# First experts of a two-block transformer layer: 24 rounds of 128 slots on 32-column strips, float32 unsplit, with an 18-slab weight ring

## Chip, cores and metric

The program runs on one core of a Trainium2 chip. The metric is the device time of one execution in microseconds; the kernel before has a median of 3347.88 us over three runs (3345.87 to 3349.38).

## What is computed

The reference is a layer of two blocks over 1024 tokens of width 1024 (256 context tokens beside them). The change is in the experts of the first block. After the mixer every token has a row of `h2`, chooses one of four groups of experts, and inside it two of eight experts:

```python
def hier_moe(h, w_rg, b_rg, w_re, b_re, w_gate, w_up, w_down):
    """h (T, D): top-1 expert group, then top-2 experts inside that group; SwiGLU experts."""
    ...
    def expert_block(args):
        xi, e = args
        return (jax.nn.silu(xi @ w_gate[e]) * (xi @ w_up[e])) @ w_down[e]
    ...
x = x + gt2 * hier_moe(h2.reshape(B * S, D), *moe_args).reshape(B, S, D)
```

There are 32 experts, each with `w_gate` and `w_up` of 1024x512 and `w_down` of 512x1024, all float32: 192 half matrices of 1 MB each. The 1024 tokens give 2048 rows of work. Block 2 (a recurrent branch, attention, and 64 experts of 256 hidden columns) follows and isn't changed.

## The kernel before, in words

The kernel is written with a tile framework that has pools of buffers and inserts the semaphore waits; its scheduler sets the order of each engine's instructions. It goes through the mixer of block 1 (`phase1a`, `phase1b`, `phase1c`), the 32 experts of block 1 (`moe1`, the place of the change), the mixer of block 2 (`phase3`) and its 64 experts (`moe2`).

**Routing.** `route_group` runs twice in `phase1c` (for token tiles 0 to 5, then 6 and 7). It gives every token-and-choice a slot number in its expert (`slot`, L832 to L833), builds one-hot rows of it (`rsl`, L859) and accumulates, with small products, a table of 96 slots x 32 experts in PSUM. `finish_table` (L876 to L881) copies it out and makes `o_tok` (token of each slot, or a negative number) and `o_w` (its weight). An expert's first 96 slots are handled in `moe1`; what lies beyond goes to `overflow`, a loop with a trip count read at run time (L1059, L1060), which is zero for these inputs: its body never runs, but all engines and DMA queues meet at a barrier there.

**Experts.** `moe1` goes through the experts one at a time, R = 96 slots each. `fetch(e)` gathers 96 rows of `h2d` into one of three buffers `m_x` (an indirect DMA of the POOL queue, L1009); `front(e)` turns them with eight transposes (L999) and splits them in two float32r parts, `m_xTh` and `m_xTl` (L1002, L1003). Weights come in slabs of 128x2048 float32 (1 MB, six to an expert: gate and up in halves of the contraction, down in halves) by DMAs of the SP queue (L1155) into a ring of 8 buffers `m_w`. `split(j)` makes two float32r parts of each slab: `m_hi` on ACT (L1179) and `m_lo` on DVE, for the second half of down on POOL (L1180); four buffers each. `mm3` then does each float32 product as three float32r products (hi x hi, lo x hi, hi x lo), 128x96 stationary (the turned rows) against 512 moving columns of the slab:

```python
    def product(out, x, w, k, o, start, stop):
        self.mm3(out[0:R], x[0][:, k, :], x[1][:, k, :], w[0][:, o:o + 512], w[1][:, o:o + 512], start, stop)
    ...
    def taken():
        j = step[0]
        step[0] += 1
        split(j + 4)
        load(j + 4 + self.M1_RING)
```

So an expert is 72 products: 48 for gate and up (`ph`), 24 for down (`py`). Silu and the product with up give `m_h` (L1254, L1255); it is turned with four transposes and multiplied with down while the next expert's gate and up run. DVE scales the result with weight and gate (`m_y`, L1226), and an indirect DMA of POOL adds its rows to `x1d` (`scatter`, L1015). After expert 20's gate and up stands `overflow`.

**After the experts**, `phase3` starts with `norms`: SP loads the gain `g`, weights `wzs` and `ws` of `w_in`, `fg` (L1444, L1280, L1448), and the rows `a_x` of `x1d` (L1451), which have to wait for the last scatter.

**moe2**, whose code stays as it is, handles two experts at a time: 64 slots of one on columns 0 to 63 of the TensorE array, 64 of the other on columns 64 to 127, in float32 unsplit (`n_w`, `n_d` the weights). In `phase1a` the small products of the modulation (`ad<-wada,cT`) put four 32-column stationary operands on the four 32-column strips of the array, float32 unsplit, in eight products to a result.

## Time and profile before

| | us |
|---|---|
| median of 3 runs | 3347.88 |
| lowest, highest run | 3345.87, 3349.38 |
| span of the profiled execution | 3342.7 |
| the execution's median beside its span | 5.2 more |
| PE busy in the span | 2993.7 (90%) |
| DVE, ACT, POOL busy | 1768.0, 1370.7, 835.8 |
| first to last product of the block-1 experts | 982.9 to about 1648 |
| `moe2` | about 2783 to the end |

The profiled execution has no run time of its own in the results; its span of 3342.7 us is taken as the median run less 5.2 us that lie around the span. A row of a view gives start or count, busy time and mean duration; "idle before" is the engine's idle time just before the instruction and who ended it. PE is the matmul part of TensorE, PEld its weight loads, SPq the queue on which SP issues DMAs.

### The profile page before, as it was taken

To read this page: it belongs to the slowest core of one execution; us is meant where nothing else is said; L and a number is where in the kernel's file an instruction comes from. 1 tells how busy PE (TensorE), PEld (TensorE's weight loads), DVE (VectorE), ACT (ScalarE), POOL (GpSimd) and SP (SyncE) were. 2 spreads that over 40 slices of the span, in tenths; PEclk is the share of its full clock that TensorE was granted. 3 is DMA by queue.
4 is the path that set the end of the run, shared out by engine and by line. 5 is a ranking of instruction groups with operands and counts; after the bars stand their busy time and mean duration, and the time that the engine had idled before them with its cause. 6 is when DMAs were issued, how large, how long until landed. Compare 5 with 4: busy or idle time off the path is not lost.

```text
span 3342.7 us, 42770 instructions
## 1 busy us (share of the span) xinstructions
PE 2993.7 (90%) x15849; PEld 2195.4 (66%) x15849; DVE 1768.0 (53%) x3374; ACT 1370.7 (41%) x2247; POOL 835.8 (25%) x553
## 2 busy tenths in 40 slices
PE   7999999799978899889799999999998997877858
PEld 4988854677756666666487778788887893332323
DVE  4244332877668778778656731348886443111101
ACT  4345311555535566566556632236664211000001
POOL 1000011122223468767510000110001103333332
PEclk8999999799989899999899999999999998999979
DMA  6223376666569899899732253332235549999988
GB/s 212 91 80 95 92 226 198 178 166 173 137 225 317 285 330 343 285 359 343 234 118 76 76 208 96 120 96 73 69 83 179 178 173 346 407 386 363 390 334 301
DMA packets 282097, 705.55 MB, mean 211 GB/s; under 512 B 33760, under 2 KB 168060, under 8 KB 233116
## 3 DMA queue, kind: packets, MB, share of 16 engines
q1 hardware_dynamic: 231036, 462.13, 42.3%
q0 software_dynamic: 44160, 222.81, 18.4%
q10 hardware_dynamic: 6688, 17.83, 1.5%
q8 instruction: 127, 2.08, 0.3%
q14 instruction: 86, 0.70, 0.1%
HBM read 616.11 MB, written 99.11 MB: 214 GB/s over the span
## 4 chain that ended last, share of the span: by engine, by line
PE 41%; DMA 17%; DVE 9%; POOL 5%; ACT 4%; issue 4%; POOLq 0%; SPq 0%; DVEq 0%; ACTq 0%
PE mm L88 31%; DMA n_d<-exp_w 13%; POOL m_lo L1180 3%; PE s L88 2%; PE tp L88 2%; ACT m_hi L1179 2%; DVE m_lo L1180 1%; DMA x1d<-m_y,o_tok 1%; PE tp L999 1%; PE o L88 1%; PE gt L88 1%; PE tp L691 1%; PE lg L88 1%; DVE da_e L660 1%; POOL m_rs L101 1%
## 5 line engine op out<-in xcount | busy, mean ns | idle before, releaser
L1180 DVE TENSOR_TENSOR m_lo<-m_w,m_hi 128x2048 fp32r<-128x2048 f32 x160 | 430.3, 2703 | 78.9 <-ACT m_hi L1179 70.3
L1179 ACT CAST m_hi<-m_w 128x2048 fp32r<-128x2048 f32 x192 | 360.6, 1907 | 84.4 <-PE mm L88 74.0
L88 PE MATMUL mm<-n_w,n_xTf 128*64 128x512 f32 x1024 | 271.6, 645 | 79.5 <-DMA n_w<-exp_w 58.1
L88 PEld LDWEIGHTS mm<-n_w,n_xTf 128*64 128x64 f32 x1024 | 92.3, 149 | 252.7 <-issue 250.3
L88 PE MATMUL mm<-m_lo,m_xTh 128*96 128x512 f32 x512 | 205.5, 401 | 20.0 <-DVE m_lo L1180 19.9
L88 PE MATMUL mm<-m_hi,m_xTh 128*96 128x512 f32 x512 | 206.9, 404 | 0.0
L88 PE MATMUL mm<-uTh,wh 128*128 128x512 f32 x512 | 205.3, 401 | 0.0
L88 PE MATMUL mm<-m_hi,m_xTl 128*96 128x512 f32 x512 | 204.4, 399 | 0.0
L88 PE MATMUL mm<-uTh,wl 128*128 128x512 f32 x512 | 203.2, 397 | 0.0
L88 PE MATMUL mm<-uTl,wh 128*128 128x512 f32 x512 | 202.4, 395 | 0.0
L88 PE MATMUL mm<-wh,hTh 128*128 128x256 f32 (+1 forms) x608 | 177.6, 292 | 2.0 <-ACT wh L269 2.0
L1284 DVE TENSOR_TENSOR wl<-ws,wh 128x512 fp32r<-128x512 f32 x128 | 91.5, 729 | 164.9 <-ACT wh L1283 152.2
L88 PE MATMUL mm<-wl,hTh 128*128 128x256 f32 (+1 forms) x608 | 175.5, 289 | 0.5 <-DVE wl L270 0.5
L88 PE MATMUL mm<-wh,hTl 128*128 128x256 f32 (+1 forms) x608 | 175.1, 288 | 0.6 <-DVE hTl L324 0.6
L1967 DVE TENSOR_TENSOR n_h<-n_h,mm 128x256 f32<-128x256 f32 x32 | 13.5, 420 | 304.4 <-ACT n_h L1966 304.4
L1180 POOL TENSOR_TENSOR m_lo<-m_w,m_hi 128x2048 fp32r<-128x2048 f32 x32 | 159.6, 4989 | 52.0 <-ACT m_hi L1179 46.3
L1009 POOL DMA_INDIRECT m_x<-h2d,o_tok x32 | 129.2, 4038 | 156.3 <-PE tp L999 129.0
L1015 POOL DMA_INDIRECT x1d<-m_y,o_tok x32 | 149.8, 4681 | 48.8 <-DVE m_y L1226 42.7
L1966 ACT ACTIVATE n_h<-mm 128x256 f32<-128x256 f32 x32 | 12.3, 384 | 327.6 <-PE mm L88 327.6
L88 PE MATMUL mm<-m_lo,m_hTh 128*96 128x512 f32 x256 | 104.3, 420 | 34.8 <-POOL m_lo L1180 34.8
L88 PE MATMUL s<-da_k,da_q 128*128 128x512 f32 (+1 forms) x384 | 115.0, 409 | 17.7 <-DVE da_e L660 17.3
L1283 ACT CAST wh<-ws 128x512 fp32r<-128x512 f32 x128 | 77.7, 619 | 127.2 <-PE mm L88 51.5
(534 smaller groups left out, 7653.4 us busy)
## 6 DMA issues: line engine op xcount, KB each, us to landing
n_w<-exp_w POOLq DMA_DIRECT2D x112, 1024.0 KB, 16.9
m_w<-expert_w_gate SPq DMA_DIRECT2D x64, 1024.0 KB
m_w<-expert_w_up SPq DMA_DIRECT2D x64, 1024.0 KB
m_w<-expert_w_down SPq DMA_DIRECT2D x64, 1024.0 KB
n_d<-exp_w POOLq DMA_DIRECT2D x58, 1024.0 KB, 16.8
wada<-w_ada SPq DMA_DIRECT2D x48, 512.0 KB
da_k<-ks SPq DMA_DIRECT2D x64, 320.0 KB
n_w<-exp_w SPq DMA_DIRECT2D x12, 1024.0 KB
```

The lines of the kernel that those rows point to most:

```text
L88: self.nc.tensor.matmul(out, l, r, start=start, stop=stop)
L101: nc.gpsimd.tensor_tensor(out, m, self.neghalf[:, 0:w], op=ALU.pow)
L660: nc.vector.tensor_scalar(e[:, c0:c0 + n], ps, 0.125, mx[:, m, b - 1:b] if b else None, op0=ALU.mult, op1=ALU.max, accum_out=mx[:, m, b:b ...
L691: nc.tensor.transpose(pt[:, i, :], e[:, ts(4 * g + i, P)], self.ident)
L999: nc.tensor.transpose(pt[:, k, :], xk[:, g + k, :], self.ident[0:rows, 0:rows])
L1009: return self.nc.gpsimd.indirect_dma_start(out=out, out_offset=None, in_=src, in_offset=bass.IndirectOffsetOnAxis(ap=idx, axis=0), bounds_ ...
L1015: return self.nc.gpsimd.indirect_dma_start(out=dst, out_offset=bass.IndirectOffsetOnAxis(ap=idx, axis=0), in_=src, in_offset=None, bounds_ ...
L1179: nc.scalar.copy(hi, w)
L1180: (nc.gpsimd if order[j][1] == 5 else nc.vector).tensor_tensor(lo, w, hi.bitcast(F32), op=ALU.subtract)
L1283: nc.scalar.copy(wh[:, r, :], st)
L1284: nc.vector.tensor_tensor(wl[:, r, :], st, wh[:, r, :].bitcast(F32), op=ALU.subtract)
L1967: nc.vector.tensor_tensor(h, h, ph[:, 1, :], op=ALU.mult)
```

## The change

The 32 experts are taken as 24 rounds of 128 slots. A round is four strips of 32 slots; strip q of round r belongs to expert `expert(r, q)`: three rounds handle four experts (one of each group of experts), three strips each. A strip's 32 turned rows are the stationary operand on 32 columns of the array, and its result lands on 32 partitions of the PSUM bank; so four experts' strips (of two different experts) stand side by side. Products are float32 unsplit (`turn_cols` with split False, no `mm3`), and `split` is gone. Experts of groups 1 and 2 are used in two rounds that follow each other, and a slab is given back after its last use (`left`). The ring has 18 slabs: 8 in the pool that held it before and 10 in the pool of `moe1`, where `m_hi` and `m_lo` lay. Gather, scatter and the DVE and ACT steps have 128 rows. The table of routing gets rows by round (`first`, `row`) and is copied out in seven pieces, on DVE and ACT in turn. `overflow` comes after round 15 of 24. Comments and docstrings are taken out, so line numbers move.

```diff
@@ route_group
+        row, rows = slot, cap
+        if "first" in out:
+            row, rows = self.t(pool, [P, 2, GT], tag="rrow")[:, :, 0:g], P
+            for k, oh in enumerate((oh0, oh1)):
+                nc.vector.tensor_tensor(tmp, oh, out["first"].unsqueeze(1).to_broadcast([P, g, E]), op=ALU.mult)
+                nc.vector.tensor_reduce(row[:, k, :], tmp, axis=AX.X, op=ALU.add)
+            past = self.t(pool, [P, 2, GT], tag="rpast")[:, :, 0:g]
+            nc.vector.tensor_tensor(row, row, slot, op=ALU.add)
+            nc.vector.tensor_scalar(past, row, 128.0, -128.0, op0=ALU.is_ge, op1=ALU.mult)
+            nc.vector.tensor_tensor(row, row, past, op=ALU.add)
+            nc.vector.tensor_scalar(past, slot, float(cap), 1000.0, op0=ALU.is_ge, op1=ALU.mult)
+            nc.vector.tensor_tensor(row, row, past, op=ALU.add)
...
-                nc.vector.tensor_scalar(sl[:, 0:cap], self.mats[:, 7, 0:cap], slot[:, k, t - t0:t - t0 + 1], None, op0=ALU.is_equal)
+                nc.vector.tensor_scalar(sl[:, 0:rows], self.mats[:, 7, 0:rows], row[:, k, t - t0:t - t0 + 1], None, op0=ALU.is_equal)
                 for u in range(nsub):
-                    self.mm(tab[u * cap:(u + 1) * cap], sl[:, 0:cap], fields[:, :, k, t - t0, u * (E // nsub):(u + 1) * (E // nsub)],
+                    self.mm(tab[u * rows:(u + 1) * rows], sl[:, 0:rows], fields[:, :, k, t - t0, u * (E // nsub):(u + 1) * (E // nsub)],
                             t == 0 and k == 0, t == NT - 1 and k == 1)
         if t1 == NT:
-            self.finish_table(pool, tab, out["tok"], out["w"], E // nsub, nsub * cap)
@@ finish_table
+        if rounds:
+            to, of = tb.rearrange("p f (j i) -> p f j i", i=3), tab.rearrange("p f (g j) -> p f j g", g=4)
+            for i, g, r0, r1 in ((0, 0, 0, 96), (0, 1, 96, 128), (1, 1, 0, 64), (1, 2, 64, 128), (2, 2, 0, 32), (2, 3, 32, 64), (2, 3, 64, 128)):
+                (nc.vector.tensor_copy if g % 2 else nc.scalar.copy)(to[r0:r1, :, :, i], of[r0:r1, :, :, g])
+        else:
+            nc.vector.tensor_copy(tb, tab[0:n])
...
@@ route_tiles
+        more = {}
+        if rounds:
+            n = 3 * E // 4
+            more["first"] = self.t(pool, [P, E], tag="o_first")
+            for g in range(4):
+                self.nc.gpsimd.memset(more["first"][:, ts(g, E // 4)], float(self.cap1 * g % P))
+        return more | {
             "cnt": self.t(pool, [P, E], tag="o_cnt"),
@@ moe1_open, moe1_load, moe1
-    M1_RING = 8
+    M1_RING = (8, 10)
     def moe1_open(self, wp):
...
-        order = [(0, 0), (0, 1)]
-        for e in range(E):
-            if e:
-                order += [(e, 0), (e, 1), (e - 1, 4), (e - 1, 5)]
-            order += [(e, 2), (e, 3)]
-        self.m1_order = order + [(E - 1, 4), (E - 1, 5)]
-        self.m1_slabs, self.m1w = {}, wp
-    def moe1_load(self, j):
+        order, before = [], None
+        for r in range(24):
+            s, i = divmod(r, 3)
+            new = [(8 * g + s) for g in ((0, 1), (2,), (3,))[i]]
+            for h in range(2):
+                order += [(e, 2 * h + j) for j in range(2) for e in new]
+                if h == 0 and before:
+                    order += [(e, 4 + j) for j in range(2) for e in before]
+            before = new
+        self.m1_order = order + [(e, 4 + j) for j in range(2) for e in before]
+        self.m1_slabs, self.m1w, self.m1_next = {}, [wp], 0
+    def moe1_load(self):
         nc, a = self.nc, self.a
...
-        e, i = self.m1_order[j]
+        e, i = self.m1_order[self.m1_next]
+        at = self.m1_next % sum(self.M1_RING)
+        self.m1_next += 1
...
-        w = self.m1_slabs[j] = self.t(self.m1w, [P, 2048], tag="m_w", bufs=self.M1_RING)
+        ring = int(at >= self.M1_RING[0])
+        w = self.m1_slabs[e, i] = self.t(self.m1w[ring], [P, 2048], tag=f"m_w{ring}", bufs=self.M1_RING[ring])
         nc.sync.dma_start(w, src.rearrange("p k n -> p (k n)"))
     def moe1(self, rt):
-        E, HID, R = 32, 512, self.cap1
+        E, HID, ROUNDS = 32, 512, 24
...
+            self.m1w.append(pool)
             gt2 = self.t(pool, [P, D], tag="gt2")
             nc.gpsimd.dma_start(gt2, self.rows[3:4, :].to_broadcast([P, D]))
-            slabs, order, load, parts, xTs = self.m1_slabs, self.m1_order, self.moe1_load, {}, {}
+            slabs, order, xTs = self.m1_slabs, self.m1_order, {}
+            left = {(e, i): 1 + (e // 8 in (1, 2)) for e, i in order}
             xbuf = []
...
-            def split(j):
-                if j >= len(order):
-                    return
-                w = slabs.pop(j)
-                hi = self.t(pool, [P, 2048], F32R, tag="m_hi", bufs=4)
-                lo = self.t(pool, [P, 2048], F32R, tag="m_lo", bufs=4)
-                nc.scalar.copy(hi, w)
-                (nc.gpsimd if order[j][1] == 5 else nc.vector).tensor_tensor(lo, w, hi.bitcast(F32), op=ALU.subtract)
-                parts[order[j]] = (hi, lo)
-            def fetch(e):
-                if e < E:
-                    self.gather(xbuf[e % 3][0:R], self.h2d, rt["tok"][0:R, e:e + 1], S - 1)
-            def front(e):
-                if e < E:
-                    xTs[e] = self.turn_cols(pool, psum, xbuf[e % 3], 8, "m_xT", True, R)
-            def product(out, x, w, k, o, start, stop):
-                self.mm3(out[0:R], x[0][:, k, :], x[1][:, k, :], w[0][:, o:o + 512], w[1][:, o:o + 512], start, stop)
...
-            def taken():
-                j = step[0]
-                step[0] += 1
-                split(j + 4)
-                load(j + 4 + self.M1_RING)
-            def gate_up(e, i, ph):
-                w = take((e, i))
+            def expert(r, q):
+                s, i = divmod(r, 3)
+                return 8 * ((4 * i + q) // 3) + s
+            def fill():
+                while self.m1_next < len(order) and (
+                        self.m1_next < sum(self.M1_RING) or not left[order[self.m1_next - sum(self.M1_RING)]]):
+                    self.moe1_load()
+            def taken(r, i):
+                for e in {expert(r, q) for q in range(4)}:
+                    left[e, i] -= 1
+                fill()
+            def fetch(r):
+                if r < ROUNDS:
+                    self.gather(xbuf[r % 3], self.h2d, rt["tok"][:, r:r + 1], S - 1)
+            def front(r):
+                if r < ROUNDS:
+                    xTs[r] = self.turn_cols(pool, psum, xbuf[r % 3], 8, "m_xT", False)
+            def gate_up(r, i, ph):
                 for k in range(4):
                     kk = 4 * (i // 2) + k
-                    product(ph[i % 2], xTs[e], w, kk, 512 * k, kk == 0, kk == 7)
-                taken()
-            def turn_h(e, h):
-                return self.turn_cols(pool, psum, h, 4, "m_hT", True, R)
-            def down(e, hT):
+                    for q in range(4):
+                        self.mm(ph[i % 2][ts(q, 32)], xTs[r][:, kk, ts(q, 32)], slabs[expert(r, q), i][:, ts(k, 512)], kk == 0, kk == 7)
+                taken(r, i)
+            def down(r, hT):
                 y = self.t(pool, [P, D], tag="m_y", bufs=2)
                 py = [self.t(psum, [P, 512], tag="mm", bufs=6) for c in range(2)]
                 for i in range(2):
-                    w = take((e, 4 + i))
                     for k in range(2):
                         for c in range(2):
-                            product(py[c], hT, w, 2 * i + k, 1024 * k + 512 * c, i + k == 0, i + k == 2)
-                    taken()
+                            for q in range(4):
+                                w = slabs[expert(r, q), 4 + i]
+                                self.mm(py[c][ts(q, 32)], hT[:, 2 * i + k, ts(q, 32)], w[:, 1024 * k + 512 * c:1024 * k + 512 * c + 512],
+                                        i + k == 0, i + k == 2)
+                    taken(r, 4 + i)
...
-                self.scatter(self.x1d, rt["tok"][0:R, e:e + 1], y[0:R])
-            for e in range(3):
-                fetch(e)
-            with tc.manual_schedule(engines={mybir.EngineType.DVE}):
-                split(0)
-                load(self.M1_RING)
-                front(0)
-                for j in range(1, 4):
-                    split(j)
-                    load(j + self.M1_RING)
+                self.scatter(self.x1d, rt["tok"][:, r:r + 1], y)
+            for r in range(3):
+                fetch(r)
+            fill()
+            front(0)
...
-                gate_up(e, 0, ph)
-                if e:
-                    hT = turn_h(e - 1, h)
-                gate_up(e, 1, ph)
-                if e:
-                    down(e - 1, hT)
-                    fetch(e + 2)
-                front(e + 1)
-                gate_up(e, 2, ph)
-                gate_up(e, 3, ph)
-                xTs.pop(e)
+                gate_up(r, 0, ph)
+                if r:
+                    hT = self.turn_cols(pool, psum, h, 4, "m_hT", False)
+                gate_up(r, 1, ph)
+                if r:
+                    down(r - 1, hT)
+                    fetch(r + 2)
+                front(r + 1)
+                gate_up(r, 2, ph)
+                gate_up(r, 3, ph)
+                xTs.pop(r)
                 h = self.t(pool, [P, HID], tag="m_h", bufs=2)
-                nc.scalar.activation(h[0:R], ph[0][0:R], AF.Silu)
-                nc.vector.tensor_tensor(h[0:R], h[0:R], ph[1][0:R], op=ALU.mult)
-                if e == 20:
+                nc.scalar.activation(h, ph[0], AF.Silu)
+                nc.vector.tensor_tensor(h, h, ph[1], op=ALU.mult)
+                if r == 15:
                     self.overflow(pool, psum, "m_", rt, self.h2d, self.x1d, wg.rearrange("e d h -> (e d) h"),
...
-            down(E - 1, turn_h(E - 1, h))
+            down(ROUNDS - 1, self.turn_cols(pool, psum, h, 4, "m_hT", False))
```

In the order of instructions the change shows at three places.

SP, around the end of `phase1c` (x1d and h2d are the last stores of the mixer, `m_w` the slabs). Before:

```order
L759 DMA x1d_1033_5561<-c_x_1947_8960 128x1024 [waits DMAHW5_49,DVE_49]
L768 DMA h2d_1034_5562<-c_h_1952_9019 128x1024 [waits DMAHW6_49,Pool_49]
L1059 TENSOR_LOAD v_ni_2649_12307 [waits DVE_49]
L1059 ISA x2
L1155 DMA m_w_1992_9182<-expert_w_gate 128x2048 [waits DMAHW7_49,DVE_49]
L1155 DMA m_w_1999_9204<-expert_w_up 128x2048 [waits DMAHW0_49,DVE_49,Activation_49]
```

Now:

```order
L759 DMA x1d_1033_5561<-c_x_1950_8976 128x1024 [waits DMAHW5_49,DVE_49]
L768 DMA h2d_1034_5562<-c_h_1955_9035 128x1024 [waits DMAHW6_49,Pool_49]
L1188 DMA m_w1_1995_9209<-expert_w_gate 128x2048 [waits DMAHW7_49,PE_49]
L1188 DMA m_w1_1996_9211<-expert_w_up 128x2048 [waits DMAHW0_49]
L1188 DMA m_w1_1997_9213<-expert_w_down 128x2048 [waits DMAHW1_49,DVE_49,DMAHW5_49,PE_49,Activation_49]
L1188 DMA m_w1_1998_9215<-expert_w_down 128x2048 [waits DMAHW6_49,DMAHW2_49]
```

The ninth slab no longer stands behind a register load that waits for the routing's last DVE step, nor for DVE's and ACT's splits; ten slabs follow the store of `h2d` directly. Up to the barrier of `overflow` SP now issues 137 of the 192 loads.

SP, at the end of the experts (`g1`, `wzs1152` and `fg` are the first loads of `phase3`, `a_x` the rows of x1d). Before:

```order
L1155 DMA m_w_3024_14032<-expert_w_down 128x2048 [waits DMAHW6_49,DVE_49]
L1444 DMA g1_3088_14319<-norm1_g_2 128x1024 [waits DMAHW7_49]
L1280 DMA wzs1152_3091_14323<-w_in_2 128x4x288 [waits DMAHW0_49]
L1280 DMA wzs1152_3092_14327<-w_in_2 128x4x288 [waits DMAHW1_49]
L1280 DMA wzs1152_3095_14333<-w_in_2 128x4x288 [waits DMAHW2_49]
L1448 DMA fg_3087_14318<-final_norm_g 128x1024 [waits DMAHW3_49]
L1280 DMA wzs1152_3096_14337<-w_in_2 128x4x288 [waits DMAHW4_49,DMAHW0_49,DVE_49]
L1451 DMA a_x_3078_14309<-x1d_1033_5561 128x1024 [waits DMASW3_49,DMAHW5_49,PE_49,Pool_49]
```

Now:

```order
L1188 DMA m_w1_2518_12906<-expert_w_down 128x2048 [waits DMAHW6_49]
L1463 DMA g1_2557_13133<-norm1_g_2 128x1024 [waits DMASW3_49,DMASW5_49,DMASW2_49,DMASW7_49,DMASW1_49,DMAHW7_49,DMASW0_49,DVE_49]
L1299 DMA wzs1152_2560_13137<-w_in_2 128x4x288 [waits DMAHW0_49]
L1299 DMA wzs1152_2561_13141<-w_in_2 128x4x288 [waits DMAHW1_49]
L1299 DMA wzs1152_2564_13147<-w_in_2 128x4x288 [waits DMAHW2_49]
L1467 DMA fg_2556_13132<-final_norm_g 128x1024 [waits DMAHW3_49,PE_49]
L1299 DMA wzs1152_2565_13151<-w_in_2 128x4x288 [waits DMAHW4_49,DMAHW0_49,DVE_49]
L1470 DMA a_x_2547_13123<-x1d_1033_5561 128x1024 [waits DMAHW5_49]
```

The wait for POOL's transfers (DMASW), the last scatter's among them, has moved from the load of `a_x` to that of `g1`, ahead of five other loads of the same queue.

PE, one quarter of a round (`m_w0` and `m_w1` are slabs of the two experts of round 1, `mm_2015` the bank of gate). Before, a quarter of an expert (`mm_2398` its bank) began:

```order
L88 MATMUL mm_2398_11101<-m_hi_2383_11031,m_xTh_2386_11045 96x512 [waits Activation_49]
L999 MATMUL tp_2419_11196<-mats_9_75,m_x2_1989_9165 128x96 [waits DMASW5_49,PE_49]
L88 MATMUL mm_2398_11101<-m_lo_2384_11032,m_xTh_2386_11045 96x512 [waits DVE_49]
L88 MATMUL mm_2398_11101<-m_hi_2383_11031,m_xTl_2387_11046 96x512
L88 MATMUL mm_2398_11101<-m_hi_2383_11031,m_xTh_2386_11045 96x512
```

Now a quarter is:

```order
L88 MATMUL mm_2015_9326<-m_w0_1949_8974,m_xTf_2011_9278 32x512 x2
L88 MATMUL mm_2015_9326<-m_w1_2001_9221,m_xTf_2011_9278 32x512 [waits DMAHW5_49]
L88 MATMUL mm_2015_9326<-m_w1_2001_9221,m_xTf_2011_9278 32x512
L88 MATMUL mm_2015_9326<-m_w0_1949_8974,m_xTf_2011_9278 32x512 x2
L88 MATMUL mm_2015_9326<-m_w1_2001_9221,m_xTf_2011_9278 32x512 x2
```

Four products of 32 columns stand one after the other, each on its own strip; PE now waits for the slab's DMA itself.

## Rows read from the trace of the kernel before

**Rows 1.** The chain of waits, in order of time: start us, us, what.

```profile
976.75 4.49 DMA m_x<-h2d,o_tok
982.89 6.99 PE mm L88 x24
...
1310.64 8.35 PE mm L88 x36
1322.29 5.08 POOL m_lo L1180
...
1330.39 8.35 PE mm L88 x36
...
1396.11 26.75 DMA x1d<-m_y,o_tok
1424.54 7.93 issue
...
1643.04 5.28 PE mm L88 x21
1650.07 8.92 DMA x1d<-m_y,o_tok
```

**Rows 2.** The page's costliest groups: busy us, mean ns of one, idle before.

```profile
L1180 DVE TENSOR_TENSOR m_lo<-m_w,m_hi 128x2048 fp32r<-128x2048 f32 x160 | 430.3, 2703 | 78.9 <-ACT m_hi L1179 70.3
L1179 ACT CAST m_hi<-m_w 128x2048 fp32r<-128x2048 f32 x192 | 360.6, 1907 | 84.4 <-PE mm L88 74.0
...
L1180 POOL TENSOR_TENSOR m_lo<-m_w,m_hi 128x2048 fp32r<-128x2048 f32 x32 | 159.6, 4989 | 52.0 <-ACT m_hi L1179 46.3
```

**Rows 3.** Stretches: us; PE, PEld, DVE, ACT, POOL busy; clock, DMA share, GB/s.

```profile
980.00:990.00 10.00, 8.62 (x35) 6.21 (x36) 7.40 (x6) 2.90 (x4) 3.06 (x3) 0.72 0.83 239
1300.00:1400.00 100.00, 92.20 (x427) 65.52 (x426) 83.13 (x56) 65.54 (x52) 81.96 (x16) 1.00 0.99 343
1430.00:1630.00 200.00, 186.69 (x862) 132.67 (x862) 164.93 (x112) 133.25 (x104) 140.42 (x28) 1.00 0.99 356
2800.00:3250.00 450.00, 345.13 (x1452) 134.03 (x1448) 54.72 (x100) 41.44 (x75) 149.62 (x199) 0.93 0.98 378
2900.00:3000.00 100.00, 77.46 (x310) 29.06 (x308) 11.73 (x21) 8.97 (x16) 32.23 (x45) 0.91 1.01 393
```

**Rows 4.** Timeline of PE in `moe2`, a pair whose weights had landed.

```profile
2795.75 3.65 PE L88 MATMUL mm<-n_d,n_hTf 128*64 128x512 f32 x16
2799.24 7.04 PE L88 MATMUL mm<-n_w,n_xTf 128*64 128x512 f32 x32
2806.20 0.71 PE L999 MATMUL tp<-mats,n_x 128*128 128x128 f32 x4
```

**Rows 5.** Tile `wada` in `phase1a`: ns min/median/max; PE's timeline of one result.

```profile
L88 PEld LDWEIGHTS ad<-wada,cT x192: 106/109/178, 12.4 to 565.3; 128*32 128x32 f32 x192
...
34.24 1.92 PE L88 MATMUL ad<-wada,cT 128*32 128x512 f32 x16
```

**Rows 6.** SP's issues in order of time; tile `m_x`, its gathers.

```profile
964.92 0.33 SPq L768 DMA_DIRECT2D h2d<-c_h  x1
980.31 0.34 SPq L1155 DMA_DIRECT2D m_w<-expert_w_gate  x1
...
DMA to landing us min/median/max: 4.5/11.5/18.1
```

**Rows 7.** Timeline of DVE at the end of routing.

```profile
975.02 0.32 DVE L876 COPY rtb<-rt 96x160 f32<-96x160 f32 x1 [0.36 <-PE rt L88]
```

**Rows 8.** The page's DMA issues: count and KB of each.

```profile
m_w<-expert_w_gate SPq DMA_DIRECT2D x64, 1024.0 KB
```

**Rows 9.** Timelines at the start of `phase3`: SP, ACT, DVE.

```profile
1619.59 0.42 SPq L1444 DMA_DIRECT2D g<-norm_g  x1
...
1655.06 1.15 ACT L1283 CAST wzh<-wzs 128x1152 fp32r<-128x1152 f32 x1 [5.93 <-DMA wzs<-w_in]
...
1656.24 1.36 DVE L1284 TENSOR_TENSOR wzl<-wzs,wzh 128x1152 fp32r<-128x1152 f32 x1 [2.65 <-ACT wzh L1283]
```

More of the change, by code (lines that the diff above doesn't have):

```diff
@@ L858, in route_group @@
                 sl = self.t(pool, [P, P], BF16, tag="rsl", bufs=4)
-                nc.vector.tensor_scalar(sl[:, 0:cap], self.mats[:, 7, 0:cap], slot[:, k, t - t0:t - t0 + 1], None, op0=ALU.is_equal)
+                nc.vector.tensor_scalar(sl[:, 0:rows], self.mats[:, 7, 0:rows], row[:, k, t - t0:t - t0 + 1], None, op0=ALU.is_equal)
                 for u in range(nsub):
-                    self.mm(tab[u * cap:(u + 1) * cap], sl[:, 0:cap], fields[:, :, k, t - t0, u * (E // nsub):(u + 1) * (E // nsub)],
+                    self.mm(tab[u * rows:(u + 1) * rows], sl[:, 0:rows], fields[:, :, k, t - t0, u * (E // nsub):(u + 1) * (E // nsub)],
                             t == 0 and k == 0, t == NT - 1 and k == 1)
         if t1 == NT:
-            self.finish_table(pool, tab, out["tok"], out["w"], E // nsub, nsub * cap)
+            if "first" in out:
+                self.finish_table(pool, tab, out["tok"], out["w"], 3 * E // 4, P, True)
+            else:
+                self.finish_table(pool, tab, out["tok"], out["w"], E // nsub, nsub * cap)
             cnt = self.t(psum, [P, NT, E], tag="rp", bufs=1)[:, 0, :]
@@ L869, in route_group, with finish_table @@
                 self.dump("d_" + n, out[n])
-    def finish_table(self, pool, tab, tok, w, E, n=P):
+    def finish_table(self, pool, tab, tok, w, E, n=P, rounds=False):
         nc = self.nc
@@ L881, in finish_table, with route_tiles @@
         nc.vector.tensor_scalar(tok, v, -128.0, None, op0=ALU.add)
-    def route_tiles(self, pool, E, nsub=1):
+    def route_tiles(self, pool, E, nsub=1, rounds=False):
         n = E // nsub
-        return {
+        more = {}
[5 more added lines that the diff above has]
+        return more | {
             "cnt": self.t(pool, [P, E], tag="o_cnt"),
@@ L943, in phase1c @@
                 if i < 4:
-                    self.moe1_load(2 * i)
-                    self.moe1_load(2 * i + 1)
+                    self.moe1_load()
+                    self.moe1_load()
             self.route_group(pool, psum, rt, lg, 32, 4, self.cap1, *groups[1])
@@ L1030, in turn @@
             if n == 8:
-                xT = self.t(pool, [P, 8, P], tag=pre + "xTf", bufs=1 if pre == "m_" else 2)
+                xT = self.t(pool, [P, 8, P], tag=pre + "xTf", bufs=2)
             else:
@@ L1183, in fetch @@
-            def fetch(e):
-                if e < E:
-                    self.gather(xbuf[e % 3][0:R], self.h2d, rt["tok"][0:R, e:e + 1], S - 1)
-            def front(e):
-                if e < E:
-                    xTs[e] = self.turn_cols(pool, psum, xbuf[e % 3], 8, "m_xT", True, R)
-            def product(out, x, w, k, o, start, stop):
-                self.mm3(out[0:R], x[0][:, k, :], x[1][:, k, :], w[0][:, o:o + 512], w[1][:, o:o + 512], start, stop)
-            step = [0]
-            def take(key):
-                assert order[step[0]] == key
-                return parts.pop(key)
@@ L1200, in taken @@
-            def taken():
-                j = step[0]
-                step[0] += 1
-                split(j + 4)
-                load(j + 4 + self.M1_RING)
-            def gate_up(e, i, ph):
-                w = take((e, i))
+            def expert(r, q):
[4 more added lines that the diff above has]
+                        self.m1_next < sum(self.M1_RING) or not left[order[self.m1_next - sum(self.M1_RING)]]):
+                    self.moe1_load()
@@ L1225, in down @@
+                    taken(r, 4 + i)
                 for c in range(2):
-                    nc.vector.scalar_tensor_tensor(y[0:R, ts(c, 512)], py[c][0:R], rt["w"][0:R, e:e + 1], gt2[0:R, ts(c, 512)],
+                    nc.vector.scalar_tensor_tensor(y[:, ts(c, 512)], py[c], rt["w"][:, r:r + 1], gt2[:, ts(c, 512)],
                                                    op0=ALU.mult, op1=ALU.mult)
-                self.scatter(self.x1d, rt["tok"][0:R, e:e + 1], y[0:R])
-            for e in range(3):
-                fetch(e)
@@ L1232, in moe1 @@
-            with tc.manual_schedule(engines={mybir.EngineType.DVE}):
-                split(0)
-                load(self.M1_RING)
-                front(0)
-                for j in range(1, 4):
-                    split(j)
-                    load(j + self.M1_RING)
+                self.scatter(self.x1d, rt["tok"][:, r:r + 1], y)
[3 more added lines that the diff above has]
+            front(0)
             h = None
-            for e in range(E):
+            for r in range(ROUNDS):
@@ L2001, in body @@
         rp = tc.tile_pool(name="rt1", bufs=1, side="right", reuse_waits="tile")
-        rt = K.route_tiles(rp.__enter__(), 32)
+        rt = K.route_tiles(rp.__enter__(), 32, 1, True)
         mp = tc.tile_pool(name="m1w", bufs=1, side="right", reuse_waits="tile")
```

6 lines of the change are left out of this document (1 added, 5 removed).

## The prediction

> **What bounds the kernel now.** I read the chain of waits first, since only what stands in it can shorten the run. In the experts of block 1 it repeats every expert: PE multiplies, then waits for POOL's 5.08 us part of the last weight split, then multiplies on; from one repetition to the next 1330.39 - 1310.64 = 19.75 us [rows 1]. The reader is to see two things there: the products, and the making of `m_lo`. The costliest groups say how much work the splitting is: 430 us on DVE, 361 on ACT, 160 on POOL [rows 2], all for the 192 slabs. Then the stretches: while DVE is 83% and POOL 82% busy, DMA is at a share of 0.99 as well, at 343 GB/s; later 356 [rows 3]. So a stage that looks bound by engines is also near its transfers, and taking the splits away alone can't give more than the transfers allow. But 343 is not all that DMA moves: in `moe2`, where DVE and ACT are at 12% and 9%, the same share of 0.98 is 378 GB/s, 393 in one stretch [rows 3]. The experts' products last from 982.9 to 1643.04 + 5.28 = 1648.3 us, with one barrier (`overflow`) of 26.75 us in the chain and 7.93 us until work runs again [rows 1].
>
> **Part 1, the products.** Before: 72 products an expert, 32 experts. Now: 24 rounds of 24 groups of four products (16 for gate and up, 8 for down). A float32 product is two matmul records. What does one set of records that stand side by side cost? In `moe2`, 32 records on two 64-column halves take 7.04 us, 16 take 3.65 [rows 4]: 16 more cost 3.39 us, 0.424 a set of two, with 0.26 us of tail. On four 32-column strips, the very form of the change, 16 records take 1.92 us [rows 5]; less the tail, 0.415 a set of four. So the trace holds four strips side by side at the price of one; I take 0.43 us. A round is 48 sets, 20.6 us, and 12 transposes (four take 0.71 us with their tail [rows 4]), 1.9 us: **22.5 us a round, 540 for 24**. Bounds: below 0.415 a set there is no row; above, 1.92 / 4 = 0.48, tail counted to each set. The runs of four strips in the trace are only 16 records long, so I keep 0.48 for the range.
>
> A rule against this: the row shows that the next set's weight loads, 0.106 to 0.109 us each [rows 5], fit into the 0.43 us. The Trainium skill (TensorE: Matmul & The Clock Gate, Part 3, "The mechanism") says a weight load overlaps running matmuls only when its row group differs, and here all four strips use all rows. By that rule each set would cost 0.43 + 0.106 us and the sum would come out on the slow side (rival 3); by the row it doesn't.
>
> **Part 2, DVE, ACT and POOL.** The splits of [rows 2] go, all 951 us of them; DVE, ACT and POOL keep copies, silu and scaling and the row transfers, a few us in each 22.5. All of these lie beside products: a round's turned rows are ready two quarters ahead, its hidden rows one quarter. I count nothing.
>
> **Part 3, the loads.** A load is 1024 KB, 1.049 MB [rows 8]; 2048 gathered and 2048 scattered rows of 4 KB add 16.8 MB to the 201.3 of the 192 loads, 8.3%. At 378 GB/s that is 1.136 / 0.378 = **3.0 us a load**, as nearest to a stage with idle DVE and ACT; ends: 2.89 (393) and 3.31 (343). The queue of the loads stays SP's, the one that moved 343, which is why I keep that end. A round needs eight loads, 24.0 us against PE's 22.5: the two are nearly equal, and the 18 slabs of lead are used up slowly. The page DMA: Bandwidth & Descriptors of the Trainium skill ("Where 436 GB/s comes from") has about 358 GB/s of HBM bind such transfers; that would be 3.17 us a load and an end some 22 us later, but the 378 over 450 us [rows 3] is above it.
>
> **Part 4, the start.** The ninth load no longer waits for the routing: SP issues it after the store of `h2d` at 964.92 instead of at 980.31 [rows 6], a gain for DMA. The first product comes later. Routing has nine more small DVE steps before its last table product, and seven copies, one after another on two engines, instead of one of 0.32 us [rows 7]. Seven at 0.3 to 0.5 with the handing over are 2 to 3.5 us, the steps, half of them in gaps, 1 to 1.5: I estimate 4 us, between 1.5 and 6. The first gather took 4.49 us on an idle DMA [rows 1]; now ten loads are in its way, and the median gather takes 11.5 [rows 6]: 9, so 4.5 more, between 0 and 7. PE has been idle for longer, and its clock was 0.72 over the first 10 us before [rows 3], between its two levels of 1.2 and 2.4 GHz: 2.5 more, between 0 and 4. First product at 982.9 + 11 = 994.
>
> **Part 5, the barrier.** It waits for every DMA that was issued ahead of it, and these are now 137 loads, up to 18 slabs ahead of PE, where the ring of 8 held it short. I keep a ledger of the ring: one load per 3.0 us, load j + 18 only after the last product on load j. Eight are there at the start; 129 x 3.0 from 968 is 1355, and full-ring pauses in the first rounds add 17: landed at 1372. PE is through round 15 at 994 + 16 x 22.5 - 6.9 = 1347 (round 0 has no down). It so stands until 1372 and about 6 us for the restart (between the 1.7 and the 7.9 of [rows 1]). Then 8 rounds and the last down: 1379 + 180 + 6.9 = **1566**. The lost 32 us replace 34.7 of before. In that time DMA stands still for 6 us only.
>
> **Part 6, the end.** Scaling and scatter stay (8.92 us [rows 1]). But the wait for POOL's transfers has moved up to the load of `g`, which before went out at 1619.59 [rows 9], some 40 us ahead of `a_x`. Behind it now queue three `wzs`, `fg`, a fourth `wzs` that needs a buffer split again, and then `a_x`, on the path: a landing like that of an idle gather (4.49 us), a cast of 1.15 and a subtraction of 1.36 [rows 1, 9] and their issue: 8 us later, between 4 and 12. From there on the order is the same: no change.
>
> **Sum.** 1566 - 1648 = -82, + 8 = **-74 us**. On the profiled span 3342.7 it gives 3268.7; the median run is 5.2 us above the span, so **3274 us**. Least: with 2.89 us a load the ledger ends at 1553, start and tail at their low ends take 10 to 14 more: 3250.
>
> **Rivals.** (1) *DMA stays at its old rate.* For it: same queue, share 0.99 at 343 to 356. Against: `moe2`. At 3.31 us a load PE waits 43 us in all and the ledger ends at 1610: -38 + 8, 3318 us. (2) *The strips lose time in long runs*, 0.48 us a set: 0.05 x 1152 sets are 58 us more, of which the wait for loads at the barrier hides 20; the ledger ends at 1604: -44 + 8, 3312 us. For it: no run of four strips over 16 records is in the trace. Against: two halves run 32 records at 0.424. (3) *Weight loads don't overlap with four strips*, the slow side: 0.43 + 0.106 = 0.536 a set, 25.7 + 1.9 = 27.6 us a round, 994 + 24 x 27.6 + 10 for the barrier (DMA is done early) = 1667: +19 + 8, 3375 us. It decides from about 0.515 us a set, where the gain is gone. For it: the trace has no long runs of four strips. Against: 1.92 us for 16 records [rows 5]. By the rule of the Trainium skill in part 1 it would be so throughout. (4) *The strips don't run side by side as said*, two at a time: 0.86 a set, ledger end 2037, some 3745 us. The 1.92 us speaks against it.
>
> **How the numbers follow.** Forecast (3274, its own range 3250 to 3295) 0.66; rival 1 0.13; rival 2 0.10; rival 3 0.06; rival 4 0.03; 0.02 for a time within 0.2% (7 us, about what a measurement of this kernel tells from no change). Faster: 0.66 + 0.13 + 0.10 = 0.89; same 0.02; slower 0.09. The range runs from 3250 to rival 1's 3318.
>
> **What would show it.** Right: 24 rounds of about 22.5 us with sets of four 0.43 us apart; no `m_hi` or `m_lo`; 370 to 390 GB/s wherever the ring has room; first product near 994; a PE gap of about 30 us after round 15, with loads landing in it; last product near 1566; `a_x` some 8 us after the last scatter has landed, behind `wzs`. Wrong: PE waiting for slabs in most rounds at under 360 GB/s (rival 1), sets over 0.45 us with slabs landed (2), 0.53 with each set starting after its weight loads (3), or POOL's row transfers or the copies in the chain, for which I counted nothing.

## The result and the profile after

The changed kernel takes 3255.45 us (median of 4 runs, 3250.73 to 3261.47) against 3346.88 us of the kernel before beside it (4 runs): a ratio of 0.973, 95% interval 0.9716 to 0.9745, 91 us less where 74 were forecast. The profiled execution of the change took 3257.55 us with a span of 3255.8 us. Against the span of before, 3342.7, that is 86.9 us less, and the four points of the prediction's sum share it out:

| us from the start | before | forecast | after |
|---|---|---|---|
| first product of the experts | 982.9 | 994 | 994.1 |
| last product of the experts | 1648.3 | 1566 | 1555.4 |
| first `a_x` landed | 1663.1 | 1589 | 1577.9 |
| end of the span | 3342.7 | 3269 | 3255.8 |

So 92.9 us come from the experts up to the last product, 7.8 go at the start of `phase3`, and behind `a_x` the two traces differ by 1.8 us.

The chain of waits, in order of time (start us, us, what); in place of [rows 1] it now has PE from the barrier to the last product, but for two DVE steps of 0.70 us at the end:

```profile
1345.72 18.23 DMA x1d<-m_y,o_tok
1363.95 1.60 issue
1365.56 26.43 PE mm L88 x224
...
1392.67 10.44 PE mm L88 x96
1403.11 1.09 PE tp L1028 x8
1404.19 10.44 PE mm L88 x96
1414.63 0.68 PE tp L1028 x4
1415.31 10.44 PE mm L88 x96
...
1548.31 7.11 PE mm L88 x64
1555.45 0.76 DVE m_y L1250
1556.21 0.27 issue
1556.47 6.33 DMA x1d<-m_y,o_tok
1563.08 0.33 SPq L1463
1563.41 0.05 issue
1563.46 5.80 DMA wzs<-w_in
1569.33 1.16 ACT wzh L1302
1570.52 1.37 DVE wzl L1303
1571.90 0.37 SPq L1299
1572.27 0.05 issue
1572.32 5.59 DMA a_x<-x1d
```

The reader is to see three things. A round is two pieces of 10.44 us and the transposes between them: 1415.31 - 1392.67 = 22.64 us. A piece is 96 records in groups of four, 24 sets, so a set takes 0.435 us. And nothing else is in a round.

The stretches (us; PE, PEld, DVE, ACT, POOL busy; clock, DMA share, GB/s), against [rows 3]:

```profile
990.00:1000.00 10.00, 7.89 (x48) 3.38 (x52) 0.69 (x1) 0.59 (x1) 0.99 (x1) 0.61 1.01 411
1200.00:1300.00 100.00, 100.00 (x887) 33.23 (x879) 15.35 (x22) 4.73 (x8) 10.52 (x8) 1.00 1.01 403
1400.00:1500.00 100.00, 100.00 (x908) 33.61 (x904) 16.01 (x23) 5.92 (x10) 11.05 (x8) 1.00 0.99 391
2710.00:3160.00 450.00, 350.03 (x1470) 135.05 (x1470) 55.96 (x101) 42.13 (x76) 150.12 (x199) 0.93 0.99 382
```

PE is busy all the time, DMA moves 403 GB/s, more than any stretch of [rows 3], and the splits of [rows 2] are gone. The share of DMA is 1.01; it was 0.99 at 343 GB/s.

Who sets the pace of the loads is in the DMA queue's own waits (SP's; line, waited for: us in total, times, longest). Before, from 1000 to 1390:

```profile
SPq L1155 <- DVE m_lo L1180: 238.4, 90, 5.8
SPq L1155 <- POOL m_lo L1180: 107.3, 19, 7.7
```

After, from 1000 to 1340:

```profile
SPq L1188 <- PE mm L88: 269.6, 68, 11.2
SPq L1188 <- DMA m_w<-expert_w_up: 9.0, 5, 2.1
```

Before, SP waited for splits in 346 of 390 us; now it waits for PE in 270 of 340, to give a slab back, and for transfers in 10. The ring is full nearly all the time. PE's own waits list none for a slab in that stretch.

### The profile page after: what moved, and what is told of

Read it like the earlier page. It is cut to its first block, busy times and chain, and to the rows that moved or that the text cites. A ratio compares the mean times of both kernels' runs of the same rounds, so it can differ in the third digit from the quotient of the medians.

```text
span 3255.8 us, 46271 instructions
## 1 busy us (share of the span) xinstructions
PE 2944.9 (90%) x18057; PEld 1958.9 (60%) x18057; DVE 1324.7 (41%) x3163; ACT 986.0 (30%) x1978; POOL 471.5 (14%) x509
## 4 chain that ended last, share of the span: by engine, by line
PE 36%; DMA 23%; issue 10%; DVE 8%; ACT 2%; POOL 2%; SPq 0%; POOLq 0%; DVEq 0%; ACTq 0%
PE mm L88 26%; DMA n_d<-exp_w 13%; DMA x1d<-m_y,o_tok 5%; PE s L88 3%; PE tp L88 2%; DMA n_w<-exp_w 1%; PE o L88 1%; PE gt L88 1%; DMA ws<-w_mla_o 1%; PE tp L691 1%; PE lg L88 1%; DVE da_e L660 1%; POOL m_rs L101 1%; DMA oTs<-od 1%; PE tp L1831 1%
## 5 line engine op out<-in xcount | busy, mean ns | idle before, releaser
L88 PE MATMUL mm<-m_w,m_xTf 128*32 128x512 f32 x3072 | 343.6, 599 | 9.7 <-issue 9.7
L88 PEld LDWEIGHTS mm<-m_w,m_xTf 128*32 128x32 f32 x3072 | 100.1, 111 | 216.9 <-issue 210.9
L88 PE MATMUL mm<-m_w,m_hTf 128*32 128x512 f32 x1536 | 171.2, 592 | 0.9 <-DVE m_hTf L1034 0.9
L1034 ACT COPY m_xTf<-tp 128x512 f32<-128x512 f32 x24 | 14.1, 586 | 426.5 <-PE tp L1028 411.3
L88 PE MATMUL mm<-n_d,n_hTf 128*64 128x512 f32 x512 | 117.0, 598 | 14.1 <-DVE n_hTf L1034 14.0
L1250 DVE SCALAR_TENSOR_TENSOR m_y<-mm,o_w,gt 128x512 f32<-128x512 f32 x48 | 36.0, 751 | 213.8 <-PE mm L88 210.9
L88 PEld LDWEIGHTS mm<-m_w,m_hTf 128*32 128x32 f32 x1536 | 51.9, 110 | 114.4 <-issue 113.7
L88 PEld LDWEIGHTS mm<-wh,hTh 128*128 128x128 f32 x608 | 116.0, 191 | 7.3 <-issue 3.7
L88 PEld LDWEIGHTS mm<-wl,hTh 128*128 128x128 f32 x608 | 116.1, 191 | 3.9 <-issue 2.0
L88 PEld LDWEIGHTS mm<-wh,hTl 128*128 128x128 f32 x608 | 115.8, 190 | 3.8 <-DVE hTl L324 1.6
```

The lines of the kernel that those rows point to most:

```text
L88: self.nc.tensor.matmul(out, l, r, start=start, stop=stop)
L1034: (nc.scalar.copy if g else nc.vector.tensor_copy)(xf[:, r, :], pt)
L1250: nc.vector.scalar_tensor_tensor(y[:, ts(c, 512)], py[c], rt["w"][:, r:r + 1], gt2[:, ts(c, 512)], op0=ALU.mult, op1=ALU.mult)
```

## The experiments

My theory: PE sets the pace of the rounds, because a load is cheaper than I took it for; the ring stays full, so at the barrier only the loads in flight are late, and that is why more was gained than forecast. Rivals: DMA is at its limit as well and only the lead hides it; the splits were what slowed DMA before.

**DMA alone.** Every second product is left out, all loads stay.

```
-                for k in range(4):
+                for k in (0, 3):
...
-                    for k in range(2):
-                        for c in range(2):
+                    for c in range(2):
```

> Leaves out every second product of the experts of block 1 (all loads stay), so that a round costs PE about 12.2 us and DMA alone sets the pace. Theory A (DMA has a reserve over the 401 GB/s that the rounds of 22.64 us ask for): 410 to 430 GB/s once the ring has run dry, rounds of 21.1 to 22.2 us, last product 1480 to 1495. Rival B (401 GB/s is all that DMA gives, PE and DMA are balanced): rounds of 22.6 us, last product near 1510. Rival C (the 378 GB/s of the prediction is the limit and the 18 slabs of lead hid it): rounds of 24 us, last product near 1530.

The stretches and SP's waits from 1100 to 1300:

```profile
1100.00:1300.00 200.00, 157.27 (x949) 46.82 (x945) 31.40 (x45) 10.65 (x18) 23.67 (x18) 0.96 1.02 406
```

```profile
SPq L1188 <- DMA m_w<-expert_w_gate: 58.6, 24, 4.3
SPq L1188 <- DMA m_w<-expert_w_up: 58.5, 22, 3.9
SPq L1188 <- DMA m_w<-expert_w_down: 50.4, 22, 3.2
SPq L1188 <- PE mm L88: 3.4, 3, 2.5
```

Here it is DMA that SP waits for, 167.5 of 200 us, and it moves 406 GB/s: 1.136 MB / 0.406 = 2.80 us a load, eight in 22.4 us. The landings say the same: 80 loads in 224.4 us, from 1086.7 to 1311.1. The rounds of the change ask for 8 x 1.136 / 22.64 = 401 GB/s. So DMA has 1% in hand, no more; that PE is the bound in the change itself is seen in SP's waits above. The 406 is below what theory A named and above rival B, and rival C, my own 378, falls. The single run took 3209.94 us, with the last product at 1503.4, between A and B. PE's rounds took some 23.1 us there, longer than the loads need and than A or B named; its order, which the fourth experiment takes up, was broken as well.

**A ring of 14.**

```
-    M1_RING = (8, 10)
+    M1_RING = (8, 6)
```

> A ring of 14 slabs instead of 18, nothing else. Theory A (DMA keeps up, the lead is not used up: slabs land 16 to 24 us before their first product, and four slabs are 11.4 us of that): no wait of PE for slabs, within 3 us of the changed kernel, perhaps 2 us faster at the barrier. Rival B (the lead is used up slowly, as the prediction had it at 3.0 us a load): 16 us of waits more, the time 5 us or more slower.

3258.39 us, ratio 0.9738 (0.9716 to 0.9761): the same. PE waits for no slab, so the lead of the last four slabs isn't needed. But two differences cancel in this time. From first to last product it is 569.4 us, 8.0 more than in the change: up to about the 12th the rounds take 22.6 us as before, the later ones up to 26.4, the one with the barrier 28.5. The next but one experiment tells why. And from the last product to `a_x` landed it is 14.3 us, 8.2 less than in the change, with `g` issued at 1528.8, ahead of the last scatter.

**The splits put back**, on a ring of 14; nobody reads the parts.

```
+                        nc.scalar.copy(hi, w)
+                        (nc.gpsimd if i == 5 else nc.vector).tensor_tensor(lo, w, hi.bitcast(F32), op=ALU.subtract)
```

> Puts the splits of the kernel before back as work that nobody reads: every slab is cast by ACT into an m_hi tile and subtracted by DVE (by POOL for the second slab of down) into an m_lo tile, on a ring of 14 slabs; to be held against the ring of 14 without them. Theory A (the work of DVE, ACT and POOL is what made packets slow before: 8 KB packets of 362 ns on average against 316 in the changed kernel): 343 to 360 GB/s in the stage, PE waits for slabs, rounds of 25.2 to 26.5 us, 35 to 75 us slower than the ring of 14. Rival B (343 GB/s before was only what the splits asked for, since SP waited 346 of 390 us for m_lo): packets stay near 316 ns, rounds stay at 22.6 to 22.9 us, within 5 us of the ring of 14.

3288.96 us, ratio 0.9828 (0.98 to 0.9855), 31 us more than the ring of 14: less than theory A's 35 to 75, more than rival B's 5. The same stretch with the splits, and without:

```profile
1200.00:1300.00 100.00, 100.00 (x902) 33.07 (x894) 86.18 (x52) 68.40 (x43) 40.11 (x15) 1.00 1.00 395
```

```profile
1200.00:1300.00 100.00, 100.00 (x882) 34.10 (x876) 16.11 (x23) 5.32 (x9) 12.44 (x10) 1.00 1.00 395
```

DVE is 86% busy instead of 16, ACT 68 instead of 5, and DMA moves the same 395 GB/s; PE waits for no slab. In this theory A is wrong. The 31 us have three parts. The first product is 11.3 us later (1001.2 against 989.9; traces of other runs with the same code up to there differ by 6 us, 988.7 to 995.1). From DVE's timeline before it, four `m_lo` stand ahead of the copy of turned rows:

```profile
986.73 8.88 DVE L1228 TENSOR_TENSOR m_lo<-m_w,m_hi 128x2048 fp32r<-128x2048 f32 x4
995.63 0.69 DVE L1034 COPY m_xTf<-tp 128x512 f32<-128x512 f32 x1
```

From first to last product it is 11.8 us more, of which PE waits 7.9 for small work of DVE. The last 8 lie between the last product and `a_x`, where `g` goes out behind the last scatter again (1590.1). So the splits cost by standing in front of small work on the same engines, not by slowing transfers, and the third part is the queue's order at the end. The 343 GB/s of before was what an expert asked for: six loads with their rows, 6 x 1.136 = 6.8 MB in 19.75 us [rows 1], are 345 GB/s.

**No barrier.**

```
-                if r == 15:
-                    self.overflow(...
```

> Leaves out the call of overflow in the experts of block 1 (its loop runs 0 times on these inputs). Theory A (PE sets the pace of the rounds, the barrier only stops PE for 12.9 us and costs 2.2 us of slow clock behind it): 24 rounds of 22.64 us without a break, last product near 1542 instead of 1555.4, 13 to 15 us faster than the changed kernel, about 3242 us. Rival B (DMA sets the pace, and the stop at the barrier is time in which it catches up): PE waits for slabs in the rounds after the 16th, the last product comes at 1550 or later, 0 to 5 us faster.

3260.1 us, ratio 0.9745 (0.972 to 0.977): no gain, against my theory. The last product came at 1559.7, in rival B's range, but not for its reason: PE waits for no slab. The stretches:

```profile
1200.00:1300.00 100.00, 100.00 (x888) 33.37 (x884) 15.64 (x23) 4.74 (x8) 10.51 (x8) 1.00 1.01 403
1400.00:1500.00 100.00, 100.00 (x824) 33.26 (x820) 14.01 (x20) 4.31 (x8) 8.41 (x6) 1.00 0.98 383
```

PE is busy throughout at full clock, but gets 824 records done in 100 us where the change does 908. The listing of PE's instructions shows why; it is the scheduler that orders them, and here it has put other products between those of a set (`m_hTf` is a down product of round 15, `mm_11542` gate of round 16):

```
L88 MATMUL mm_11596<-m_w_2279_11393,m_hTf_11564 32x512 x3
L88 MATMUL mm_11597<-m_w_2279_11393,m_hTf_11564 32x512 x3
L1028 MATMUL tp_11639<-mats_75,m_x_1994_9198 128x128 x2
L1028 MATMUL tp_11645<-mats_75,m_x_1994_9198 128x128 x4
L88 MATMUL mm_11542<-m_w_2271_11314,m_xTf_11494 32x512
L88 MATMUL mm_11596<-m_w_2280_11395,m_hTf_11564 32x512
```

Three strips go without their fourth, whose slab is another expert's. PE's timeline of the same kernel (start us, us):

```profile
1374.68 8.35 PE L88 MATMUL mm<-m_w,m_xTf 128*32 128x512 f32 x63
```

63 records in 8.35 us are 3.3 to each 0.43 us instead of 4. Taking records that start together for a set, the 4608 records of the rounds stand in 1194 sets here, in 1156 in the change, where 1152 full ones would do. On the ring of 14 there were 1196, the first broken ones at 1274, well ahead of its barrier: so a barrier doesn't by itself keep the order. The next run fixes the order.

**No barrier, and the written order on PE.**

```
+            with tc.manual_schedule(engines={mybir.EngineType.PE}):
                 for r in range(ROUNDS):
```

> As the kernel without overflow in the experts of block 1 (0 iterations left out), and PE keeps the written order in the rounds. There the rounds behind the 15th took 23.5 to 25.6 us instead of 22.64, with PE busy all the time and products of four strips taken apart into groups of two and three. Theory A (that order, not DMA, ate what the stop had cost): all rounds 22.64 us, last product near 1542, 12 to 14 us faster than the changed kernel, about 3242 us. Rival B (DMA held the rounds back, and PE's order only shows it): rounds stay at 24 to 25 us behind the 15th with waits for slabs, last product 1555 to 1560, no faster.

3242.1 us, ratio 0.9681 (0.9664 to 0.9698), as theory A has it. All rounds behind the first take 22.64 us, the last product comes at 1543.1, 548.0 us behind the first; in the change it was 561.3. The barrier costs **13.3 us**: in the change's own trace PE idles there for 11.0 us and the slow clock takes 2.2 more (its four sets too many, 1.7 us, and an end 1.7 us shorter cancel). The order ate 18.3 us in the run before (566.3 us from first to last product), which is its 42 sets too many at 0.435 us.

```profile
1367.54 10.51 PE L88 MATMUL mm<-m_w,m_xTf 128*32 128x512 f32 x96
1377.98 0.75 PE L1028 MATMUL tp<-mats,m_h 128*128 128x128 f32 x4
```

**The tail.** In `norms` the tiles that are loaded early lie where weight slabs lay.

```
+        fg = self.t(pool, [P, D], tag="fg")
+        g1 = self.t(pool, [P, D], tag="g1")
+        for i in range(3):
+            self.t(pool, [P, 1152], tag="wzs1152", bufs=3)
...
         xs = [self.t(pool, [P, D], tag="a_x", bufs=3) for t in range(3)]
```

> In norms the tiles of fg, g1, wzs and wz are laid out ahead of a_x and a_u, so that the loads of g, wzs and fg fall on weight slabs that PE left long before, and a_x takes the place that waits for the scatters. Theory A (what the tail lost is the order behind the last scatter: a_x went out 9.0 us after the scatter's landing, behind g, four wzs, a cast and a subtraction): g and wzs are issued around 1512, a_x within 1 us of the last scatter's landing, 8 to 10 us faster than the changed kernel, about 3246 us, last product unchanged at 1555. Rival B (the work behind a_x waits for the wz parts or fg anyway): 0 to 4 us faster.

```profile
1548.99 1.34 PE mm L88 x14
...
1551.38 8.38 DMA x1d<-m_y,o_tok
...
1559.97 0.34 SPq L1472
...
1560.41 4.63 DMA a_x<-x1d
```

`g` goes out at 1515.9, `a_x` 0.2 us behind the scatter. From the last product to `a_x` landed it is 14.7 us (1550.33 to 1565.04), 22.5 in the change: 7.8 us less, as before the change. The whole run, 3250.82 us and 0.9708 (0.969 to 0.9726), is 4.6 us lower, less than theory A had, and the interval doesn't tell it from the change; the piece in the trace does. In that trace first and last product come 5 us earlier, which the edit doesn't touch, and from the last product to the end it is 1697.8 us, against 1700.4 in the change and 1697.1 in the kernel without the barrier, whose tail is the old one. So the piece is shown; that its gain lasts to the end isn't.

**The barrier where PE idles.** `overflow` ahead of the first gather, the written order on PE, nothing left out.

```
+            self.overflow(pool, psum, "m_", rt, self.h2d, self.x1d, ...
             for r in range(3):
                 fetch(r)
```

> Nothing left out: overflow stands ahead of the first gather instead of behind round 15, where PE idles anyway and at most two loads are in flight, and PE keeps the written order in the rounds. Theory A (the stop costs what is in flight, and a written order keeps four strips together): first product 994 to 999, 24 rounds of 22.64 us, last product 1542 to 1547, no gap, 8 to 13 us faster than the changed kernel, about 3245 us. Rival B (DMA's reserve is too small: eight slabs now start behind the stop, some 20 us later, and the lead runs out): PE waits for slabs in the first ten rounds, last product 1552 or later, within 4 us of the changed kernel.

3247.0 us, ratio 0.9693 (0.9675 to 0.9711). No gap, rounds of 22.64 us, 547.7 us from first to last product, 13.6 less, and 8.5 us less for the whole run. But the gather goes out at 991.0 instead of 983.0 and the first product comes at 1001.7, later than I allowed: some 7 us go back, and the last product comes at 1549.4 instead of 1542 to 1547. Rival B falls: the lead lasts.

**All three together, and once more with the gathers ahead of the barrier.**

> The early overflow, the written order on PE and the new layout in norms together. Theory A (the three costs are separate and lie one behind the other on the path): last product 1542 to 1547, a_x within 1 us of the last scatter's landing, 17 to 22 us faster than the changed kernel, 3234 to 3239 us. Rival B (they share a cause, or what follows gives it back): less than 12 us faster.

3247.01 us, ratio 0.9701 (0.9681 to 0.9721), its runs from 3241.99 to 3256.92: 8.4 us less than the change, no more than the early barrier with the written order gave alone, so rival B. The trace, one of its faster executions (3243.39 us), has the first product 7.1 us later, the products 16.4 us shorter and the piece up to `a_x` some 6 shorter, in all 15 us. `g` goes out only at 1546.1 here, behind the last product, not at 1515.9 as in the tail experiment.

> As the kernel with the early overflow, the written order on PE and the new layout in norms, but the first three gathers are issued ahead of overflow instead of behind it; nothing left out. Theory A (with the early stop the first gather went out at 990.6 instead of 983.0, and the first product came at 1001.2 instead of 994.1; the gathers can lie inside the stop): first product 992 to 997, rounds as before 22.64 us, last product 1537 to 1542, 5 to 8 us faster than with the gathers behind it, 17 to 22 us faster than the changed kernel run beside it. Rival B (the stop now waits for the gathers themselves, which have loads in their way): first product 1000 or later, no faster than with the gathers behind.

```profile
987.03 1.33 PE L1028 MATMUL tp<-mats,m_x 128*128 128x128 f32 x5 [7.34 <-DMA m_x<-h2d,o_tok]
998.59 0.90 PE L1028 MATMUL tp<-mats,m_x 128*128 128x128 f32 x3 [10.23 <-issue]
999.42 8.92 PE L88 MATMUL mm<-m_w,m_xTf 128*32 128x512 f32 x60
```

> The changed kernel itself once more, beside the last version on the same chip, so that the two ratios to the kernel before share its runs. Both theories: a ratio of 0.971 to 0.975, last product within 6 us of 1555, rounds of 22.64 us, 13 to 14 us lost at the stop behind round 15.

3242.23 us, ratio 0.9684 (0.9669 to 0.97), against 3253.61 and 0.9717 (0.9703 to 0.973) for the changed kernel on the same chip: 11 us less, with nothing left out, where theory A had 17 to 22; the intervals just part. The first gather has landed by 987, but the barrier also stands behind the two others and the loads beside them, and the first product is still at 999.4: rival B, for the most part. Which of these it waits for longest wasn't tried.

## Why the prediction was right, and where its sizes were off

**Bounds.** Right that the splits held the chain. Wrong that DMA at a share of 0.99 was near its limit: 343, 403 and 406 GB/s all go with 0.99 to 1.02. The view that tells is what SP waits for. The Trainium skill (Perfetto Trace Analysis, Identifying the Most-Contended Engine) warns that DMA's occupancy misleads; this case agrees, with these three numbers.

**Part 1.** 0.435 us a set against 0.43, 22.64 us a round against 22.5: right. Sets are 0.435 apart with weight loads of 110 ns among them, PEld 33% and PE 100% busy, so loads lie beside products. The rule of the Trainium skill (TensorE: Matmul & The Clock Gate, Part 3, "The mechanism"), by which a weight load overlaps only when its row group differs, isn't borne out; a sentence ahead of it in that section also allows the background weight buffer.

**Part 2.** Right: no copy or scaling stands in a round's chain.

**Part 3 is the term that was mis-sized.** 3.0 us a load, where DMA alone takes 2.80. I kept 3.31 us as the queue's old rate, though 343 GB/s was only what the splits asked for. And I took `moe2`'s average of 378 for what DMA gives anywhere. It wasn't demand: POOL's queue, which issues the loads there, waits for landings in 203 of 450 us (2800 to 3250, before the change) and for PE in 19. But one slice of 84 us had 407 GB/s already before:

```profile
POOL n_w L1911 <- DMA n_w<-exp_w: 125.3, 78, 2.4
POOL n_d L1914 <- DMA n_d<-exp_w: 77.4, 35, 2.6
```

```profile
2841.30:2924.90 83.60, 67.27 (x278) 25.57 (x276) 10.98 (x20) 8.29 (x15) 27.70 (x38) 0.92 1.02 407
```

Why `moe2` moves less on average isn't shown. At 3.0 DMA has 24.0 us of work in a round and eats the lead; at 2.80 it has 22.4, PE is the bound, and the lead stays.

**Part 4.** First product 994.1 against 994, and that close by luck. The gather goes out 6.3 us later than before (983.03; 4 forecast) and takes 9 us (9 forecast). The clock over the first 10 us was 0.61, but up to the first product only 0.5 us more were lost, where I had 2.5; the cost shows behind it, where the first 64 records take 8.89 us instead of 7.07. And the same kernel profiled again had its first product at 990.4.

**Part 5.** The mechanism held, its size followed part 3. The timeline of PE at the barrier:

```profile
1345.61 7.07 PE L88 MATMUL mm<-m_w,m_xTf 128*32 128x512 f32 x64
1353.57 0.74 PE L1028 MATMUL tp<-mats,m_h 128*128 128x128 f32 x4 [0.88 <-DVE m_h L1274]
...
1365.56 9.27 PE L88 MATMUL mm<-m_w,m_xTf 128*32 128x512 f32 x64 [9.74 <-issue]
```

Short stretches there, as above, and POOL's timeline:

```profile
1358.00:1362.00 4.00, 0.00 (x0) 0.00 (x0) 0.00 (x0) 0.00 (x0) 0.00 (x0) 0.70 0.62 251
1362.00:1366.00 4.00, 0.44 (x4) 0.38 (x8) 0.67 (x1) 0.59 (x1) 0.00 (x0) 0.50 0.01 4
```

```profile
1356.09 1.04 POOL L1038 DMA_INDIRECT m_x<-h2d,o_tok  x1 [7.43 <-PEq L1089]
```

PE stops at 1352.7, transfers end at 1362, among them a gather issued as late as 1356.09, and PE goes on at 1365.6: 12.9 us, where I had 32 (loads landed at 1372 instead of 1362, 6 us of restart instead of 3.6). The clock had fallen to 0.50, and the next 64 records took 9.27 instead of 7.07 us. So the stop was over 13.4 us earlier than forecast (1379), and the rounds behind it, with that clock and 0.14 us more each, took 2.9 us longer: the last product came 10.6 us earlier.

**Part 6.** +7.8 us against +8, by the very queue that was named, `g`, `wzs`, a split and `a_x`; the tail experiment takes it away. But the two numbers agree in part by luck: from the scatter's landing to that of `a_x` it is 11.1 us more (15.1 against 4.1), and 3.3 come back because the last scaling and scatter are shorter (7.4 against 10.7), which I hadn't counted.

**Around the span.** I put 5.2 us between the span and the median run. In the runs that list both, the two differ by 1.8 (3257.55 against 3255.8); so the profiled execution of before will have been some 3.4 below its median. Of the 18.5 us between 3274 and 3255.45, 12.9 lie in the span, 3.4 in this term, and 2.1 in that the profiled execution of the change was slower than its median.

**Rivals.** 1 (343 GB/s), 2 (0.48 us a set), 3 and 4: none came. What the list lacked is that PE's order itself can cost: the change depends on four products standing together. Behind the barrier that I priced as a loss they did, and without it they didn't, though on the ring of 14 the barrier kept nothing together.

## What to carry to other kernels

Read a transfer limit from what the issuing queue waits for, not from a busy share: a queue that waits for buffers shows demand; one that waits for landings shows what DMA gave in that stage, here 378 in `moe2` and 406 in the rounds, and such a figure needn't hold for the next stage. Where speed comes from several products side by side, look at the order in which they are issued after every edit, and fix it by hand. Before a barrier is taken away, look at the order behind it; where it must stay, put it where the engine idles and little is in flight.

## What the runs showed of the hardware that I had not expected

- A group of fewer strips costs what four cost: with 3.3 records to a 0.43 us slot instead of 4, PE was 100% busy in both cases (824 and 908 records in 100 us), and 42 sets too many cost 18.3 us.
- One core's DMA moved 406 GB/s with nearly every wait on landings (167.5 us, 3.6 on others). The Trainium skill (DMA: Bandwidth & Descriptors, "Where 436 GB/s comes from") has about 358, half of what two cores share, bind such transfers; no long stretch of the rounds shows that bound.
- DVE, ACT and POOL at 86, 68 and 40% left DMA at 395 GB/s, as at 16, 5 and 12%. Why 8 KB packets took 360 ns on average before the change and 321 after it (1000 to 1340 us) stays open: with the splits put back it was 329, on the ring of 14 without them 326.
